# An encoder layer's step from recurrence to attention: one normalisation woven into the attention's maxima, with TensorE in program order from there

## The chip, the core and the metric

The kernel runs on one core of one Trainium2 chip. A core has TensorE (matrix products into PSUM; its weight loads are listed apart, as PEld), VectorE (DVE), ScalarE (ACT), GpSimd (POOL) and SyncE (SP), which issues most transfers. Each engine works off its own queue in order; semaphores join them. The metric is the device time of one execution in microseconds, lower is better.

## The reference

One layer of a hybrid encoder for 1024 prompt frames (positions 0 to 1023, no history) and 64 sample frames (with a recurrent state and 256 cached keys):

```python
proj = (rms_norm(x) * (1 + sc1) + sh1) @ w_in          # 1024 -> 3336 columns
r, k, v, decay, a, g = rwkv part of proj               # 8 heads x 64, token-shifted
y = rwkv_scan(...)                                     # delta rule, state 64 x 64 a head
mu, var = mean and variance of y over each head's 64 channels
y = (y - mu) * rsqrt(var + GN_EPS) * gn_g + gn_b
y_rwkv = (y + bonus) * g                               # g = sigmoid(dg) @ w_gate_up
q, kf, vf, logf = fox part of proj                     # 8 heads x 64
y_fox = softmax(q @ k.T / 8 + lc_q - lc_k, causal) @ v # lc: running sum of logf
x = x + gt1 * (concat(y_rwkv, y_fox) @ w_out)
x = x + gt2 * ((silu(h2 @ w_ffn_gate) * (h2 @ w_ffn_up)) @ w_ffn_down)
```

Everything is float32; most products are made of three products of a high and a low part.

## The kernel before, in words

Channels lie on the 128 partitions and frames along the free axis. Frames are worked in two halves (`halves`): the first has 512, the second 512 and the 64 samples. Eight heads are four pairs, `j` 0 to 3, two heads to a tile of 128 partitions.

`phase` makes the projections of a half and the recurrent part, in an order that a string (`ORDER`) writes out. `rwkv_b` (B) makes the recurrence: from one chunk of 64 frames to the next there is a chain of a matmul `pS` (L663) and two small evacuations of it, `sv` on VectorE (L666) and on ScalarE (L667); the outputs `pY` are copied into `y`, one head by ScalarE and one by VectorE (L672). `rwkv_n` (N, L677 on) normalises a pair: the mean by a matmul with `bmean` (`pbs`, L405), a subtraction on VectorE (L683), a square on ScalarE, the variance by another matmul, Ln and Exp on ScalarE, two operations of VectorE (L691, L692), the gate `g` by a matmul `plora` (L398), its product with `y` on VectorE (L693), and a DMA that GpSimd issues into the scratch `yscr` (L695). The pair 3 of the second half is the last; its normalisation stands behind the phase, as code of its own.

Attention follows. For each pair of heads of one half:

- `att_max` makes the approximate scores of each block of 128 queries against all keys that it may see (`pmx`, two halves of 512 keys at most, with a matmul of a mask `cmask` by the identity `identr` on the diagonal block) and takes their maxima on VectorE (L1022, `nmx` or `pc`). Its generator yields after each such piece.
- `att_rows` transposes the maxima (`pnm`, L1032) and writes them into rows of the query operand by two operations of VectorE, one a head (L1035), so that the scores come out with the maxima subtracted.
- `att_main` goes over the blocks of keys: the exact scores `pst` (two or three matmuls), Exp on ScalarE (L1064), sums over the blocks in `acc` (head 0 on VectorE, head 1 on GpSimd when `te.on` is set, L1077 to L1080), the products with the values `pav`, at the end the sum over keys `psm` and the division (L1147 to L1149). For samples there are the small `pss` and `pvs`.

`att_main` yields between its pieces, and the caller fills in pieces of other generators: the maxima of the next pair (`fill(mx, ...)`), the first half's attention (`low_steps`), the output projection `po`. `self.te` wraps TensorE: with `te.on` each matmul keeps the place that the code gives it; without, the scheduler may move it. In the profile its matmuls stand at L1906, its transposes at L1909. Before, `te.on` is set only in `att_second`, so the maxima and scores of pair 0 of the first half, and the maxima of pair 0 of the second half (both in `run`), are placed by the scheduler, between the recurrence's last steps and the last normalisation.

PSUM in this part has banks by tag: `mx` 2, `st` 3, `mm` 2, `pv` 1. For the first half's pairs 1 to 3 (`pair_bufs` with `big` false) the value products, the sums `psm` and the transposed maxima `pnm` share the two `mm` banks.

Operands of the first half's pairs lie in tiles that are free at that time: pair 1 in `mixfh`/`mixfl`, pair 2 in `mixrh`/`mixrl`, pair 3 in `mixr1`. GpSimd clears half of the rows of each (`aux_rows`, L890), then SyncE loads the rest (`pair_load`, L973). The rows of the second half's pair 1 are `kb1` and `q1`.

`att_consts` makes `identr`, two `cmask` and four `nmx` behind the phases: a cast on VectorE (L874), memsets and a select on GpSimd, two casts on VectorE (L883).

## Time and profile before

| | |
|---|---|
| runs, us | 1680.83, 1672.7, 1681.77 (median 1680.83) |
| the profiled execution: its own time, its span | 1676.35 us, 1674.7 us |
| mean granted clock of TensorE | 0.988 |
| TensorE busy | 1617.9 us, 97% of the span |
| VectorE, ScalarE, GpSimd busy | 63%, 39%, 12% |
| chain that ended last | TensorE 79%, VectorE 10%, ScalarE 5%, DMA 3% |

The recurrence's end, the last normalisation and pair 0 of the first half lie from about 660 to 700 us of the span, the second half's attention with the first half's pairs from 700 on, the output projection's filling from 786 on, and the rest of the layer behind 880. A table of windows gives for each stretch of the span the busy time of each engine, TensorE's granted clock (PEclk, 1 is full), the DMA engines' busy share and the rate. A table of waits gives who stood idle for whom: in total, how often, the longest. A timeline gives start, duration, engine, line, operation and, in brackets, the idle time ahead.

### The profile page before, as it was taken

The page shows a single profiled execution, that of the slowest core. Times are in us where ns is not written, and L with a number is a line of the kernel's source. Part 1 is how long each engine was busy: PE and PEld are TensorE (multiplying, and loading weights), DVE is VectorE, ACT ScalarE, POOL GpSimd, SP SyncE. Part 2 cuts the span into 40 slices and gives each one's busy share as a digit, 9 for nine tenths or more (in the row PEclk, how much of TensorE's full clock was granted, in tenths as well). Part 3 has the DMA queues.
Part 4 walks back from the last instruction along what each step waited for, and adds up shares of the span by engine and source line. Part 5 has one row for each costly group of instructions (what it writes and reads, how often), then busy time and mean ns, then how long its engine had stood idle before and what let it go on. Part 6 is the DMA issues. An engine that isn't in the chain of part 4 may idle for free.

```text
span 1674.7 us, 31845 instructions
## 1 busy us (share of the span) xinstructions
PE 1617.9 (97%) x12783; PEld 1397.8 (83%) x12783; DVE 1060.0 (63%) x2162; ACT 659.9 (39%) x1284; POOL 197.6 (12%) x336
## 2 busy tenths in 40 slices
PE   6999999999999999899999999999999999999999
PEld 3666777788888887555669899999999999999998
DVE  6576686757876653666668965555555556545545
ACT  4543565653545445234346632222333233211210
POOL 1101101030211013434441000000000000000000
PEclk9999999999999999899999999999999999999999
DMA  8535467531233244754434432222222226323313
GB/s 311 163 101 133 117 181 202 168 90 43 62 86 96 80 109 114 219 145 153 142 118 163 160 105 77 78 78 78 78 78 78 78 65 210 132 73 98 100 40 123
DMA packets 126738, 197.80 MB, mean 118 GB/s; under 512 B 60734, under 2 KB 67550, under 8 KB 126590
## 3 DMA queue, kind: packets, MB, share of 16 engines
q1 hardware_dynamic: 124862, 190.10, 37.3%
q0 software_dynamic: 1728, 5.67, 0.9%
q8 instruction: 100, 1.64, 0.4%
q14 instruction: 48, 0.39, 0.1%
HBM read 152.54 MB, written 43.19 MB: 117 GB/s over the span
## 4 chain that ended last, share of the span: by engine, by line
PE 79%; DVE 10%; ACT 5%; DMA 3%; issue 2%; SPq 1%; POOL 0%; DVEq 0%; ACTq 0%; POOLq 0%
PE pd L1548 16%; PE pfe L1433 8%; PE pfc L1433 8%; PE pfa L1433 8%; PE pmm L324 4%; PE pmm L326 4%; PE pfb L1433 4%; PE pmm L325 4%; PE po L1906 3%; PE pst L1906 2%; PE pbs L405 2%; PE pav L1906 2%; PE pmx L1906 2%; PE pS L663 1%; DVE wlo L246 1%
## 5 line engine op out<-in xcount | busy, mean ns | idle before, releaser
L324 PE MATMUL pmm<-hhi,whi 128*128 128x288 f32 (+1 forms) x624 | 218.7, 351 | 3.9 <-ACT pb L347 3.9
L325 PE MATMUL pmm<-hlo,whi 128*128 128x288 f32 (+1 forms) x624 | 216.6, 347 | 0.6 <-DVE hlo L302 0.6
L326 PE MATMUL pmm<-hhi,wlo 128*128 128x288 f32 (+1 forms) x624 | 213.5, 342 | 0.0
L242 ACT CAST whi<-wraw 128x1024 fp32r<-128x1024 f32 (+2 forms) x116 | 99.1, 855 | 222.3 <-PE pd L1548 165.0
L1548 PE MATMUL pd<-al,whi 128*128 128x512 f32 (+1 forms) x528 | 172.4, 327 | 0.0
L1548 PE MATMUL pd<-ah,wlo 128*128 128x512 f32 (+1 forms) x528 | 172.2, 326 | 0.0
L1548 PE MATMUL pd<-ah,whi 128*128 128x512 f32 (+1 forms) x528 | 172.2, 326 | 0.0
L1552 DVE SCALAR_TENSOR_TENSOR x1t<-pd,mod,x1t 128x512 f32<-128x512 f32 x192 | 91.4, 498 | 109.5 <-PE pd L1548 108.7
L324 PEld LDWEIGHTS pmm<-hhi,whi 128*128 128x128 f32 x624 | 119.1, 191 | 19.6 <-ACT pb L347 5.1
L325 PEld LDWEIGHTS pmm<-hlo,whi 128*128 128x128 f32 x624 | 119.1, 191 | 12.0 <-issue 1.7
L326 PEld LDWEIGHTS pmm<-hhi,wlo 128*128 128x128 f32 x624 | 118.6, 190 | 10.7 <-issue 1.7
L246 DVE TENSOR_TENSOR wlo<-wraw,whi 128x1024 fp32r<-128x1024 f32 (+2 forms) x108 | 104.8, 970 | 28.7 <-ACT whi L242 28.4
L1548 PEld LDWEIGHTS pd<-ah,whi 128*128 128x128 f32 x528 | 99.0, 188 | 7.1
L1548 PEld LDWEIGHTS pd<-ah,wlo 128*128 128x128 f32 x528 | 99.0, 188 | 7.1
L1548 PEld LDWEIGHTS pd<-al,whi 128*128 128x128 f32 x528 | 99.1, 188 | 7.0
L1433 PE MATMUL pfc<-hh,hS 128*128 128x256 f32 (+1 forms) x352 | 102.3, 291 | 1.2 <-ACT hh L1335 1.2
L1433 PE MATMUL pfc<-hh,lS 128*128 128x256 f32 (+1 forms) x352 | 102.3, 291 | 0.0
L1433 PE MATMUL pfa<-hh,whi 128*128 128x256 f32 (+1 forms) x352 | 101.8, 290 | 0.0
L1433 PE MATMUL pfa<-hl,whi 128*128 128x256 f32 (+1 forms) x352 | 101.8, 289 | 0.0
L1433 PE MATMUL pfa<-hh,wlo 128*128 128x256 f32 (+1 forms) x352 | 101.6, 289 | 0.0
L1433 PE MATMUL pfc<-hl,hS 128*128 128x256 f32 (+1 forms) x352 | 101.1, 287 | 0.0
L1380 ACT CAST hS<-wraw 128x512 fp32r<-128x512 f32 x88 | 53.6, 619 | 62.9 <-PE pfc L1433 62.0
(458 smaller groups left out, 4107.3 us busy)
## 6 DMA issues: line engine op xcount, KB each, us to landing
wraw<-in_w_in_dram SPq DMA_DIRECT2D x52, 512.0 KB
wada<-in_w_ada_dram SPq DMA_DIRECT2D x48, 512.0 KB
as<-actscr SPq DMA_DIRECT2D x22, 544.0 KB
wraw<-in_w_gate_dram SPq DMA_DIRECT2D x22, 512.0 KB
wraw<-in_w_up_dram SPq DMA_DIRECT2D x22, 512.0 KB
wraw<-in_w_down_dram SPq DMA_DIRECT2D x40, 256.0 KB
wraw<-in_w_out_dram SPq DMA_DIRECT2D x16, 512.0 KB
actscr<-sg SPq DMA_DIRECT2D x22, 288.0 KB
```

Of the source, the lines that this page charges most:

```text
L242: nc.scalar.copy(hi, src)
L246: eng.tensor_tensor(lo, src, hi.bitcast(F32), op=ALU.subtract)
L324: nc.tensor.matmul(ps[0:M, 0:n], whi[:, k, 0:M], xhi[:, k, off:off + n], start=(k == 0), stop=False)
L325: nc.tensor.matmul(ps[0:M, 0:n], whi[:, k, 0:M], xlo[:, k, off:off + n], start=False, stop=False)
L326: nc.tensor.matmul(ps[0:M, 0:n], wlo[:, k, 0:M], xhi[:, k, off:off + n], start=False, stop=(k == kt - 1))
L405: nc.tensor.matmul(ps[:, 0:n], w, x[:, off:off + n], start=True, stop=True)
L663: nc.tensor.matmul(ps, kb[:, c], sv[:, c], start=True, stop=True)
L1380: nc.scalar.copy(w[x][0], src)
L1433: nc.tensor.matmul(ps, l[:, k], r[:, s, k], start=(first and k == 0 and y == 0), stop=(k == 3 and y == 2), skip_group_check=True)
L1548: nc.tensor.matmul(ps[:, 0:n], w[:, i], x[:, t:t + n], start=(i == 0 and y == 0), stop=(i == len(fs) - 1 and y == 2))
L1552: nc.vector.scalar_tensor_tensor(dst, ps[:, so - off:so - off + l], self.mod[:, 40 + o, b:b + 1], dst, op0=ALU.mult, op1=ALU.add)
L1906: return self.pin(self.tc.nc.tensor.matmul(*a, **k))
```

## The change

The last normalisation becomes a generator, `rwkv_n_last`, whose three steps `run` takes at chosen places: the gate's product first (after the sixth piece of the first maxima), copied by ScalarE into a tile `glate`; then the mean and the square; then the variance and the rest. Its product with the gate goes from VectorE to GpSimd, and its matmuls go through `te`, in the `mm` banks. `te.on` is set at the end of the last phase, ahead of the first maxima. The maxima of the second half's pair 0 are filled in one a step (before: two after each whole block). In `rwkv_b` both heads of `y` of the last pair are copied by ScalarE. `att_consts` is called twice: inside the last phase for pair 0 of the first half, and behind the phases with three copies by ScalarE; its `nmx` are cleared by VectorE instead of GpSimd. For the first half's pairs the transposed maxima `pnm` take an `mx` bank instead of an `mm` one. In `low_steps` the next pair's maxima start one block sooner and come one a step, where they came two at a time. `mixfh` and `mixfl` are placed ahead of `mixrh` and `mixrl` in their pool.

```diff
@@ rwkv_b
-            for h, cp in enumerate((nc.scalar.copy, nc.vector.tensor_copy)):
+            for h, cp in enumerate((nc.scalar.copy, nc.scalar.copy if hf.smp and j == 3 else nc.vector.tensor_copy)):
...
+    def rwkv_n_last(self, hf, j, part, sgd):
...
+        def product(w, x):
+            for off, m in hf.chunks:
+                ps = self.ps([P, 512], tag="mm", name="pn3")
+                self.te.matmul(ps[:, 0:m], w, x[:, off:off + m], start=True, stop=True)
+                yield slice(off, off + m), ps[:, 0:m]
+        g = self.zpool.tile([P, 576], F32, tag="z", name="glate")
+        for c, ps in product(self.wg[:, j * P:(j + 1) * P], sgd):
+            nc.scalar.copy(g[:, c], ps)
+        yield
+        for c, ps in product(self.bmean, y):
+            nc.vector.tensor_tensor(y[:, c], y[:, c], ps, op=ALU.subtract)
+        rs = self.slot(name="gsq", tag="sb")
+        nc.scalar.activation(rs[:, 0:n], y[:, 0:n], AF.Square)
+        yield
+        for c, ps in product(self.bmean, rs):
+            nc.scalar.activation(rs[:, c], ps, AF.Ln, bias=self.eps_g)
+        nc.scalar.activation(rs[:, 0:n], rs[:, 0:n], AF.Exp, scale=-0.5)
+        nc.vector.scalar_tensor_tensor(y[:, 0:n], y[:, 0:n], col(V_GG), rs[:, 0:n], op0=ALU.mult, op1=ALU.mult)
+        nc.vector.scalar_tensor_tensor(y[:, 0:n], y[:, 0:n], col(V_GB), bon[:, 0:n], op0=ALU.add, op1=ALU.add)
+        nc.gpsimd.tensor_tensor(y[:, 0:n], y[:, 0:n], g[:, 0:n], op=ALU.mult)
+        self.late_q.dma_start(self.yscr[hf.i][:, j], y[:, 0:n])
+        yield
...
@@ att_consts
+        if src:
+            c["m"] = [ap.tile([P, 3 * P], F32R, name=f"cmask{x}") for x in range(2)]
+            for d, t in zip((c["id"], *c["m"]), (src["id"], *src["m"])):
+                nc.scalar.copy(d, t)
...
-            nc.gpsimd.memset(t, 0.0)
+            nc.vector.memset(t, 0.0)
...
@@ pair_bufs
-                                                {"pv": "mm", "sm": "mm", "dn": "mm"})
+                                                {"pv": "mm", "sm": "mx", "dn": "mm"})
...
@@ low_steps
-                    fill(mx, 2 * (last > 1))
+                    fill(mx, last > 0)
...
                 else:
+                    fill(mx, last > 0)
                     last = b + 1
...
@@ run
-            for b, f in late.values():
-                f(b())
...
-            for _ in self.att_max(0, halves[0], self.g0):
-                pass
+            self.te.on = True
+            (n3,) = late.values()
+            mx, fill = self.att_max(0, halves[1], g), lambda n: [next(mx, None) for _ in range(n)]
+            for i, _ in enumerate(self.att_max(0, halves[0], self.g0)):
+                if i == 5:
+                    next(n3)
             self.att_rows(0, halves[0], self.g0)
-            mx, fill = self.att_max(0, halves[1], g), lambda n: [next(mx, None) for _ in range(n)]
             for b in self.att_main(0, halves[0], self.g0):
-                fill(2 if isinstance(b, int) else 1 if b != "v" else 99)
+                if b in (0, 1, 2):
+                    next(n3, None)
+                fill(1 if b != "v" else 5)
+            fill(99)
...
-            mine = {x: rows4(p, halves[0], x) for x in ("mixrh", "mixrl", "mixfh", "mixfl")}
+            mine = {x: rows4(p, halves[0], x) for x in ("mixfh", "mixfl", "mixrh", "mixrl")}
```

The order of the instructions moves at three places of which the prediction speaks. (The lines' numbers differ between the two programs: L1948 and L1951 after are L1906 and L1909 before, both inside the `te` wrapper.) The first is TensorE at the end of pair 0's first maxima; `kbf`, `qf`, `kaf`, `qaf` are the first half's operands, `kb` and `q` the second half's, `z` and `wg` make the gate. Before:

```order
L1906 MATMUL pmx<-kbf,qf 128x512
L405 MATMUL pbs<-gsq,bmean 128x288
L1906 MATMUL pmx<-cmask_8106,identr 128x256
L405 MATMUL pbs<-gsq,bmean 128x288
L1909 MATMUL pnm<-ident,nmx_8117 64x128
L398 MATMUL plora<-z,wg 128x288
L1906 MATMUL pst<-qf,kbf 128x512
L1906 MATMUL pst<-cmask_8114,identr 128x256
```

After, from the same `pnm` on:

```order
L1951 MATMUL pnm<-ident,nmx_7563 64x128
L1948 MATMUL pst<-qaf,kaf 128x512
L1948 MATMUL pst<-qf,kbf 128x512
L1948 MATMUL pst<-cmask_7560,identr 128x256
L1948 MATMUL pmx<-kb_8112,q_8113 128x512
L1948 MATMUL pst<-qaf,kaf 128x512
L1948 MATMUL pst<-qf,kbf 128x512
L1948 MATMUL pst<-cmask_7560,identr 128x256
L1948 MATMUL pmx<-kb_8112,q_8113 128x256
L1948 MATMUL pmx<-cmask_8096,identr 128x256
L1948 MATMUL pn_8213<-y,bmean 128x288
L1948 MATMUL pn_8216<-y,bmean 128x288
```

The normalisation's products (`pbs` before, `pn` after) no longer stand between the first maxima; they come behind the first scores, with the second half's maxima between them.

The second place is TensorE in the first half's pair 2, where the maxima of pair 3 (`pmx` from `mixr`) are filled in between its scores (`pst` from `mixrl` and `mixrh`). Before, behind the scores of blocks 0 and 1:

```order
L1906 MATMUL pmx<-mixr_8365 128x256
L1906 MATMUL pmx<-cmask_8106,identr 128x256
L1906 MATMUL pmx<-mixr_8365 128x256
L1906 MATMUL pmx<-cmask_8106,identr 128x256
L1906 MATMUL pst<-mixrl_8382 128x256
L1906 MATMUL pst<-mixrh_8381 128x256
L1906 MATMUL pst<-cmask_8114,identr 128x256
L1906 MATMUL pmx<-mixr_8365 128x384
L1906 MATMUL pmx<-cmask_8106,identr 128x256
L1906 MATMUL pmx<-mixr_8365 128x512
L1906 MATMUL pmx<-cmask_8106,identr 128x256
L1909 MATMUL pnm<-ident,nmx_8120 64x128
```

After, from the scores of block 1 (384 wide) on:

```order
L1948 MATMUL pst<-mixrl_8394 128x384
L1948 MATMUL pst<-mixrh_8393 128x384
L1948 MATMUL pst<-cmask_8097,identr 128x256
L1948 MATMUL pmx<-mixr_8375 128x256
L1948 MATMUL pmx<-cmask_8096,identr 128x256
L1948 MATMUL pst<-mixrl_8394 128x384
L1948 MATMUL pst<-mixrh_8393 128x384
L1948 MATMUL pst<-cmask_8097,identr 128x256
L1948 MATMUL pmx<-mixr_8375 128x256
L1948 MATMUL pmx<-cmask_8096,identr 128x256
L1948 MATMUL pmx<-mixr_8375 128x384
L1948 MATMUL pmx<-cmask_8096,identr 128x256
```

The maxima begin at block 1 instead of block 2, mostly one at a time.

The third place is GpSimd between the clearing of pair 3's rows (`mixr`) and that of the second half's pair 1 (`kb`). Before:

```order
L890 MEMSET mixr_8365 64x1024 x2
L1077 COPY acc<-pt 128x128 x2
L695 DMA yscr_72<-y 128x576
L890 MEMSET mixfh_8383 64x1024 x2
L890 MEMSET mixrh_8381 64x1024 x2
L890 MEMSET kb_8407 64x2688
```

After:

```order
L924 MEMSET mixr_8375 64x1024 x2
L1113 COPY acc<-pt 128x128 x2
L1114 TENSOR_TENSOR acc<-pt 128x384
L1116 TENSOR_TENSOR acc<-acc,pt 128x256
L723 TENSOR_TENSOR y<-y,glate 128x576
L724 DMA yscr_72<-y 128x576
L1116 TENSOR_TENSOR acc<-acc,pt 128x128
L924 MEMSET mixfh_8391 64x1024 x2
L924 MEMSET mixrh_8393 64x1024 x2
L924 MEMSET kb_8417 64x2688
```

Three additions of head 1 (`te.on` now holds for them) and the product with the gate stand ahead of the clearing that the loads of pair 1 and of `kb1` wait for.

On VectorE the cast of `identr` (L874), which stood between the fourth and fifth `sv` of the last recurrence, goes to pair 2's recurrence some 60 us earlier; in its place stand four memsets of 128x64. On ScalarE three copies (128x128 and twice 128x384) and one copy of `y` come in at the same point.

More of the change, by code (lines that the diff above doesn't have):

```diff
@@ L695, in rwkv_n @@
         self.late_q.dma_start(self.yscr[hf.i][:, j], y[:, 0:n])
+    def rwkv_n_last(self, hf, j, part, sgd):
+        nc, vc, n = self.nc, self.vc, hf.n
+        col = lambda base: vc[:, base + j:base + j + 1]
+        y, bon = part
+        def product(w, x):
[20 more added lines that the diff above has]
+        yield
     def ones_rows(self):
@@ L869, in cache_kv, with att_consts @@
         self.put_split(kf, j, SP + SS, PAST, 1)
-    def att_consts(self, ap):
+    def att_consts(self, ap, n, src=None):
         nc = self.nc
-        self.identr = ap.tile([P, P], F32R, name="identr")
-        nc.vector.tensor_copy(self.identr, self.ident)
-        self.cmask = []
-        for x in range(2):
+        c = {"id": ap.tile([P, P], F32R, name="identr"), "m": []}
+        if src:
+            c["m"] = [ap.tile([P, 3 * P], F32R, name=f"cmask{x}") for x in range(2)]
+            for d, t in zip((c["id"], *c["m"]), (src["id"], *src["m"])):
+                nc.scalar.copy(d, t)
+        else:
+            nc.vector.tensor_copy(c["id"], self.ident)
+        for x in range(0 if src else 2):
             cm = self.slot([P, P], name="cm")
@@ L880, in att_consts @@
                                     pattern=[[2 * x - 1, P]], channel_multiplier=1 - 2 * x)
-            self.cmask.append(ap.tile([P, 3 * P], F32R, name=f"cmask{x}"))
-            nc.gpsimd.memset(self.cmask[x].bitcast(F32), 0.0)
-            nc.vector.tensor_copy(self.cmask[x][:, P:2 * P], cm)
-        self.nmx = [ap.tile([P, 64], F32, name=f"nmx{x}") for x in range(4)]
-        for t in self.nmx:
-            nc.gpsimd.memset(t, 0.0)
+            c["m"].append(ap.tile([P, 3 * P], F32R, name=f"cmask{x}"))
+            nc.gpsimd.memset(c["m"][x].bitcast(F32), 0.0)
+            nc.vector.tensor_copy(c["m"][x][:, P:2 * P], cm)
+        c["nmx"] = [ap.tile([P, 64], F32, name=f"nmx{x}") for x in range(n)]
+        for t in c["nmx"]:
+            nc.vector.memset(t, 0.0)
+        return c
     def aux_rows(self, kb, *rest):
@@ L921, in pair_bufs @@
     def pair_bufs(self, g, big):
+        g["c"] = self.ac
         for n, m in (("pt", 512), ("acc", 512), ("r", 512), ("fy", 576)):
@@ L1001, in att_max @@
         nc, te = self.nc, self.te
-        nmx = self.nmx[2 * hf.i + j % 2]
+        c_ = g["c"]
+        nmx = c_["nmx"][(2 * hf.i + j % 2) % len(c_["nmx"])]
         kb, qc = g["kb"], g["q"]
@@ L1017, in att_max @@
                         e, m2 = (0, SS) if smp else (max(0, d - P), 256)
-                        te.matmul(ps[0:qn, e:e + m2], self.identr[0:qn, 0:qn],
-                                  self.cmask[0][0:qn, P - d + e:P - d + e + m2], start=False, stop=True,
+                        te.matmul(ps[0:qn, e:e + m2], c_["id"][0:qn, 0:qn],
+                                  c_["m"][0][0:qn, P - d + e:P - d + e + m2], start=False, stop=True,
                                   skip_group_check=True)
@@ L1031, in att_rows @@
         pt = self.ps([64, P], tag=g["tags"]["sm"], name="pnm")
-        te.transpose(pt, self.nmx[2 * hf.i + j % 2], self.ident)
+        te.transpose(pt, g["c"]["nmx"][(2 * hf.i + j % 2) % len(g["c"]["nmx"])], self.ident)
         for h in range(2):
@@ L1060, in scores @@
                 if diag:
-                    te.matmul(ps[:, w:w + 256], self.identr, self.cmask[1][:, P - c0 + w:P - c0 + w + 256], start=False,
+                    te.matmul(ps[:, w:w + 256], g["c"]["id"], g["c"]["m"][1][:, P - c0 + w:P - c0 + w + 256], start=False,
                               stop=True, skip_group_check=True)
@@ L1111, in att_main @@
                     te.matmul(ps[:, h, x], kb[h][:, kc], qb[h][:, 512:576], start=False, stop=x < 2, skip_group_check=True)
-                te.matmul(ps[:, h, 2], self.identr, self.cmask[1][:, P:P + SS], start=False, stop=True,
+                te.matmul(ps[:, h, 2], g["c"]["id"], g["c"]["m"][1][:, P:P + SS], start=False, stop=True,
                           skip_group_check=True)
@@ L1614, in phase @@
             r[j] = (lambda p=p: p, lambda p, j=j: self.rwkv_n(hf, j, p, zg))
-        return r
+        return {j: self.rwkv_n_last(hf, j, p, zg) for j, p in y.items()} if hf.smp else r
     def run(self):
@@ L1706, in early @@
                 rws.close()
-                self.g0 = self.pair_first(E(at0, "att0"))
+                p = E(at0, "att0")
+                self.ac = self.att_consts(p, 1)
+                self.g0 = self.pair_first(p)
                 for x in range(2):
@@ L1737, in run @@
             with tc.high_priority():
-                self.att_consts(R(att, "attc", 1))
+                self.ac = self.att_consts(R(att, "attc", 1), 4, self.ac)
             self.pkeys = {}
```

3 lines of the change are left out of this document (1 added, 2 removed).

## The prediction

> **What bounds the kernel now.** I read the page first.
>
> ```profile
> span 1674.7 us, 31845 instructions
> PE 1617.9 (97%) x12783; PEld 1397.8 (83%) x12783; DVE 1060.0 (63%) x2162; ACT 659.9 (39%) x1284; POOL 197.6 (12%) x336
> ```
>
> TensorE is busy 97% of the span, so the change, which adds no product and takes none away, can only win idle time of TensorE or time at a lower clock. Where those lie, a table of windows around the change tells (time, then busy time of TensorE, its weight loads, VectorE, ScalarE, GpSimd; granted clock; DMA share; GB/s).
>
> ```profile
> 600.00:665.90 65.90, 65.31 (x641) 56.17 (x641) 25.03 (x49) 35.51 (x83) 10.31 (x12) 1.00 0.42 111
> 665.90:700.10 34.20, 26.80 (x125) 16.60 (x123) 25.59 (x55) 10.65 (x25) 21.30 (x31) 0.97 0.71 193
> 700.10:711.20 11.10, 10.01 (x38) 8.28 (x39) 5.59 (x12) 2.88 (x5) 0.96 (x1) 0.64 1.04 277
> 711.20:734.20 23.00, 22.60 (x121) 15.30 (x122) 17.94 (x34) 8.35 (x17) 8.76 (x10) 1.00 0.42 130
> 734.20:766.00 31.80, 25.46 (x134) 14.41 (x133) 16.95 (x33) 12.53 (x27) 7.94 (x10) 0.89 0.52 154
> 766.00:880.00 114.00, 112.66 (x593) 78.26 (x593) 71.26 (x93) 45.76 (x88) 52.76 (x44) 1.00 0.43 141
> ```
>
> Ahead of 665.9 and behind 766 TensorE is full (65.31 of 65.90; 112.66 of 114.00). Between them it idles 34.20 - 26.80 = 7.4 us in the second row and 31.80 - 25.46 = 6.3 us in the fifth, and the clock falls in the second, third and fifth. What is won there passes on to the end, because the work behind is TensorE's own. Next the waits of TensorE, from 665 to 712 and then from 712 to 768 (total, times, longest), the small ones left out:
>
> ```profile
> PE pS L663 <- ACT sv L667: 2.5, 2, 2.2
> PE pmx L1906 <- DVE pc L1022: 1.5, 4, 0.7
> PE pss L1906 <- DVE q L1035: 0.8, 1, 0.8
> PE pnm L1909 <- DVE nmx L1025: 0.7, 1, 0.7
> ```
>
> ```profile
> PE pmx L1906 <- DVE nmx L1022: 2.2, 5, 0.7
> PE psm L1906 <- DVE mixr L1035: 1.6, 1, 1.6
> PE psm L1906 <- DVE mixrh L1035: 1.0, 1, 1.0
> PE pnm L1909 <- DVE nmx L1022: 0.8, 1, 0.8
> PE pss L1906 <- DVE nmx L1022: 0.8, 1, 0.8
> ```
>
> It is VectorE that ends nearly every one: its maxima and the rows made of them. Last, the windows in which the clock was at half:
>
> ```profile
> 697.90:708.10 10.20, 8.70 (x32) 7.44 (x33) 4.95 (x12) 1.68 (x3) 0.00 (x0) 0.50 1.04 245
> 749.10:752.50 3.40, 3.40 (x10) 0.98 (x10) 1.64 (x2) 0.00 (x0) 0.00 (x0) 0.50 0.41 89
> 759.30:762.70 3.40, 3.40 (x13) 2.25 (x14) 0.58 (x2) 1.82 (x4) 1.04 (x1) 0.50 0.79 236
> ```
>
> Each follows a run of waits. At half clock half of the busy time is lost: 4.35, 1.7 and 1.7 us.
>
> **Part by part.** *The masks.* The rows: VectorE's casts, GpSimd's memset, TensorE's `pS` behind them.
>
> ```profile
> 665.46 2.25 DVE L874 CAST identr<-ident 128x128 fp32r<-128x128 f32 x1
> 671.53 0.21 DVE L883 CAST cmask<-cm 128x128 fp32r<-128x128 f32 x1
> 665.29 2.33 POOL L890 MEMSET kb<- 64x2688 f32 x1 [11.87 <-PE pmm L326]
> 668.41 0.49 PE L663 MATMUL pS<-sv,kr 128*128 128x128 f32 x2 [2.24 <-ACT sv L667]
> 728.29 0.49 ACT L1064 ACTIVATE pt<-pst 128x384 f32<-128x384 f32 x1 [4.72 <-PE pst L1906]
> 728.88 0.28 ACT L1064 ACTIVATE x<-pst 128x128 f32<-128x128 f32 x1
> ```
>
> Two casts of one shape took 2.25 and 0.21 us; the long one began during GpSimd's memset and ended 0.09 us behind it (667.71 against 667.62), and the recurrence stood 2.24 us for it. The cast goes. ScalarE takes three copies in its place, by its nearest rows 0.28 + 2 x 0.49 = 1.26 us, ahead of the next `sv`, so I keep 1.0 us of 2.24. Bounds: 2.2 if ScalarE's gaps hide the copies; 1.0 us lost if the four new memsets of VectorE stand behind GpSimd's as the cast did. I take **-1.0**. The earlier masks, 60 us ahead, lie beside TensorE's projections (first row above) and cost nothing; uncovered, they would be one GpSimd memset, about 1 us. The Trainium skill (SBUF — State Buffer, Who interferes with whom) says that casts and copies of VectorE in two-port modes, and its operations with two SBUF inputs against GpSimd's reads, wait for GpSimd's whole instruction, while a VectorE memset does not on trn2; the cast agrees, no row here shows the memset. By it the memsets are free and the term stays.
>
> *First maxima, normalisation, second maxima.* Of the 7.4 us idle 2.5 were the recurrence; 4.9 are left. The normalisation's steps now lie between scores and maxima, so neither VectorE nor TensorE meets them in the chain; VectorE also loses two copies of `y`, the product with the gate and head 1's additions. The two `psm`, which stood apart, become neighbours:
>
> ```profile
> 688.87 1.07 PE L1906 MATMUL psm<-acc,ones 128*64 128x512 f32 x2
> 735.47 1.08 PE L1906 MATMUL psm<-x,ones 128*64 128x512 f32 x4 [0.99 <-DVE mixrh L1035]
> 693.55 0.68 DVE L1149 TENSOR_TENSOR fy<-pav,r 128x512 f32<-128x512 f32 x1
> ```
>
> One head alone took 1.07, both together 1.08, so 1.0 us of TensorE goes. The tail stays: the last maximum to `pnm` 0.7, to the rows 0.8, and `fy` (0.68) now comes between the two rows; with 0.6 that I leave for small waits for VectorE, 2.8 stay. So 4.9 + 1.0 - 2.8 = **-3.1**; bounds 0 (the pinned queue meets as many waits as it had) and -5.2.
>
> *The first half-clock stretch.* 4.35 us; with fewer waits ahead of it I let one third of its length come back: **-2.9**, bounds 0 and -4.35.
>
> *GpSimd and the loads.* Three additions and the gate's product come ahead of the clearing of `mixfh`, `mixrh` and `kb1`, and SyncE's queue stands behind that.
>
> ```profile
> 758.95 1.40 POOL L246 TENSOR_TENSOR mixfl<-fy,mixfh 128x576 fp32r<-128x576 f32 x1 [2.30 <-ACT mixfh L242]
> 687.37 1.84 POOL L890 MEMSET mixfh<- 64x1024 f32 x2
> 694.73 1.12 SPq L973 DMA_DIRECT2D kb<-kx  x2
> 711.23 0.47 PE L1906 MATMUL pmx<-kb,q 128*128 128x512 f32 x1
> mixfl<-qx SPq DMA_DIRECT2D x1, 512.0 KB
> v<-vtok SPq DMA_DIRECT2D x2, 512.0 KB
> q<-qx SPq DMA_DIRECT2D x3, 288.0 KB
> kb<-kx SPq DMA_DIRECT2D x3, 672.0 KB
> ```
>
> The clearing follows `y`'s last product, before and after. That product takes 1.40 us on GpSimd by its nearest row, and its steps, behind two scores now, come some 1.6 us later: together 3, so the clearing starts near 690.4 instead of 687.37 and `kb1` is issued near 698 instead of 694.73. How long a load then takes is in no row; the transfers were saturated (1.04) at 277 GB/s, and from `mixfl` (two of 512 KB) over `v` and `q1` to `kb1` 2.5 MB are issued, some 9 us, so I estimate that `kb1` landed near 700 and will land near 703.5. TensorE needs it at 711.23 now, without a wait, and 7 to 8.5 us sooner then (the terms above): 703 to 704. A wait of **+1.0**, bounds 0 and 4. The other order of the tiles in their pool has its price in the same term.
>
> *One block sooner, and the `mx` bank.* 6.3 us idle in the fifth row: 2.2 + 0.8 + 0.8 for maxima that came two at a time with two banks, 1.6 and 1.0 for `psm`, which stood until VectorE had read `pnm` out of the other `mm` bank. Spread singly, most of the first go; in an `mx` bank `pnm` holds up nobody that comes within 1.4 us. 0.7 stays, and 1.0 comes new in pair 1, where VectorE is busy 17.94 of 23.00 us and gets more maxima: **-4.6**, bounds -2 and -6.
>
> *The other two half-clock stretches.* They follow these waits: 3.4 us, of which I take **-2.6**, bounds 0 and -3.4.
>
> Sum: -1.0 - 3.1 - 2.9 + 1.0 - 4.6 - 2.6 = -13.2 us. The profiled execution took 1676.35 us, 1.65 above its span; that gives 1663.1. It lies 4.5 below the median of the three runs and inside them (1672.7 to 1681.77); the mean of the four is 1677.9, and from that I forecast **1665**.
>
> **Rivals.** *The clock does not follow.* The stretches began at 697.9, 749.1 and 759.3: 51.2 and 10.2 us apart, 15 and 3 times 3.4, and they last 10.2, 3.4 and 3.4. So the gate looks at fixed pieces of 3.4 us, and ahead of the first the waits were small, at most 1.5 us (the first table's four of `pmx`). If such small waits suffice, those that I leave do too: no clock term, -13.2 + 5.5 = -7.7, and without the load's wait -8.7: 1669. The Trainium skill (TensorE: Matmul & The Clock Gate, What's actually happening) gives the same window, 3413 ns, free-running, but throttles after an idle window; none of these was idle, so the trace agrees with the length and not with the condition. By its rule idle gaps this short would decide nothing, and the time would be the same 1669. Chance 0.22.
>
> *The loads become the bound: slower.* GpSimd's additions and VectorE's two-input operations stand for each other:
>
> ```profile
> 723.24 1.45 DVE L1080 TENSOR_TENSOR x<-x 128x256 f32<-128x256 f32 x1
> 733.45 0.42 DVE L1080 TENSOR_TENSOR acc<-acc,pt 128x256 f32<-128x256 f32 x1
> 720.61 0.29 PE L1906 MATMUL pmx<-mixrh 128*128 128x256 f32 x1
> ```
>
> The same addition took 1.45 beside GpSimd's and 0.42 alone. Four such meetings ahead of the clearing put it past 694, `kb1` to 709 and `mixrh` behind it to 716, while TensorE, pinned, wants them at 703 and 711: it stands 6 and 5 us with everything queued behind, and the clock falls again as often as now, with one piece more (1.7). -1.0 - 3.1 + 11 - 4.6 + 1.7 = +4: 1682. It decides if the first clearing of `mixfh` begins later than 694. For it: the saturated queue; against: no wait on a load now, with 11 us to spare at `kb1`. Chance 0.10.
>
> *The gains are given back.* The pinned order meets a wait of VectorE at nearly each maximum (bounds 0 and -2 of the two idle terms), clocks half won: -1 - 2 + 1 = -2: 1676. Chance 0.10.
>
> **How the numbers follow.** The forecast keeps 0.58, with 1656 to 1671 of its own: its best bounds (-2.2 - 5.2 - 4.35 - 6 - 3.4 = -21) give 1657 from the mean, its worst reach the rivals. The range 1656 to 1676 adds the clock's rival and half of the last. A measurement can tell about 0.5%, 8.4 us: faster means below 1669.5. The forecast lies there but for 0.04, and of the clock's rival 0.13 of its 0.22: 0.67 faster. Slower than 1686.3 is the far side of the loads' rival, with 0.05. The rest, 0.28, is the same.
>
> **What would show it.** Right: `pS` with no wait over 1.3 us; the first `pss` from `q` and `kb` near 696; half-clock time under 8 us in place of 17; no wait of `psm` for L1035; TensorE busy over 95% from 734 on. Wrong: a wait of `pmx` for a load of `kb1` or `mixrh` over 4 us; the clearing of `mixfh` behind 694; idle time from 665 to 766 still over 10 us.

## The result and the profile after

The changed kernel takes 1667.38 us (median of 15 executions), the kernel before 1677.53 (15 executions): a ratio of 0.994, interval 0.9928 to 0.9952, 10.2 us less. Two of the fifteen executions of the changed kernel took 3879 us, at a granted clock of 1.00 in their records; no profile of them is kept, so their cause is open, and the ratio and its interval leave them out. 1665 was forecast, 1656 to 1676 as the range. The profiled execution of the changed kernel is one of 1667.38 us. Its page begins:

```profile
span 1665.7 us, 31855 instructions
PE 1610.5 (97%) x12783; PEld 1396.0 (84%) x12783; DVE 1056.6 (63%) x2159; ACT 662.4 (40%) x1292; POOL 202.5 (12%) x336
```

TensorE makes the same 12783 products and is busy 7.4 us less, in a span that is 9.0 us shorter: most of the gain is not idle time, but products that ran faster or stood closer. The table of windows of the changed kernel, with edges at the same products as the six rows of the prediction (columns as there):

```profile
600.00:667.76 67.76, 66.87 (x656) 57.54 (x657) 26.33 (x58) 35.57 (x85) 11.75 (x15) 1.00 0.45 117
667.76:697.99 30.23, 23.29 (x125) 15.86 (x125) 21.44 (x44) 13.04 (x31) 22.44 (x25) 1.00 0.69 186
697.99:710.90 12.91, 10.58 (x41) 8.23 (x42) 7.72 (x16) 3.44 (x6) 2.40 (x4) 0.74 1.04 285
710.90:732.42 21.52, 20.49 (x109) 14.00 (x111) 15.47 (x31) 8.32 (x18) 8.10 (x9) 1.00 0.47 181
732.42:758.35 25.93, 23.94 (x146) 14.22 (x141) 17.11 (x32) 10.80 (x24) 7.98 (x10) 0.93 0.59 166
758.35:873.45 115.10, 112.92 (x594) 78.20 (x593) 72.93 (x95) 46.82 (x90) 53.08 (x44) 1.00 0.44 140
```

The second row lost 4 us and the fifth 5.9; the third, at half clock for half of its length (0.74), became longer (12.91 for 11.10), and still has 2.3 us of idle time. Idle time in rows two to five is 6.94 + 2.33 + 1.03 + 1.99 = 12.3 us, where it was 7.4 + 1.1 + 0.4 + 6.3 = 15.2. TensorE's waits from 660 to 712, and then from 705 to 768 (total, times, longest):

```profile
PE pnm L1951 <- DVE nmx L1058: 2.9, 3, 1.3
PE pS L663 <- ACT sv L667: 1.8, 2, 0.9
PE pss L1948 <- DVE q L1071: 1.5, 2, 0.9
PE pmx L1948 <- DVE pc L1058: 1.0, 2, 0.7
PE pmx L1948 <- DVE mixfh L1071: 0.7, 1, 0.7
```

```profile
PE pmx L1948 <- DVE nmx L1058: 1.5, 4, 0.7
PE pnm L1951 <- DVE nmx L1058: 1.4, 2, 1.1
PE pss L1948 <- DVE nmx L1058: 0.8, 1, 0.8
```

The 2.2 us wait of `pS` and both of `psm` are gone; `pnm` and `pss` wait longer than before. Last the clock: two stretches at half are left of three, each with the piece of 3.41 us ahead of it:

```profile
696.29:699.70 3.41, 1.47 (x11) 1.25 (x11) 2.70 (x4) 0.64 (x2) 2.78 (x4) 1.00 1.04 410
699.70:706.53 6.83, 6.82 (x24) 5.73 (x25) 2.68 (x7) 1.69 (x3) 0.05 (x1) 0.50 1.05 259
750.90:754.32 3.42, 2.64 (x20) 2.23 (x19) 2.10 (x4) 2.77 (x8) 0.56 (x2) 1.00 0.32 79
754.32:757.73 3.41, 3.41 (x14) 1.29 (x14) 2.19 (x3) 1.29 (x3) 1.31 (x1) 0.50 0.90 299
```

The stretch near 700 is 6.8 us (10.2 before), all of it busy; those at 749 and 759 became one of 3.4.

For all kernels below I measure one stretch between two products that every one of them makes: from the recurrence's 130th `pgT` (655.04 us of the span before, 656.90 after) to the second product of `po` (786.69 and 780.13). It took 131.65 us before and 123.23 after: 8.4 us less. The time outside it changes from run to run by the clock: ahead of that `pgT` the fourteen profiles of this study have between 10.2 and 30.7 us at half clock (20.5 before, 23.9 after), and it comes between 651.1 and 659.0 us. A difference of 2 or 3 us between two total times says little here; the stretch says more. But each kernel has one profile, and one half-clock piece more or less (1.7 us) can come by chance in the stretch too: the changed kernel and the first two runs below have the same products up to the second half's `pnm`, the same idle time there (6.1 us), and took 39.8, 41.4 and 41.4 us to it, because in the last two a piece of 3.41 us at half clock fell into it.

| kernel | median us (executions) | ratio to before, interval | stretch, us | idle in it | half clock in it |
|---|---|---|---|---|---|
| before | 1677.53 (15) | | 131.65 | 15.4 | 17.1 |
| changed | 1667.38 (15) | 0.994, 0.9928 to 0.9952 | 123.23 | 13.3 | 10.2 |
| wide products in the waits | 1663.35 (6) | 0.9915, 0.9887 to 0.9943 | 122.52 | 11.9 | 6.8 |
| narrow products in the waits | 1666.20 (10) | 0.9936, 0.9916 to 0.9957 | 123.27 | 11.3 | 10.2 |
| sooner maxima and bank alone | 1672.79 (12) | 0.9979, 0.9956 to 1.0002 | 126.97 | 13.2 | 13.6 |
| without these two | 1674.93 (12) | 0.9983, 0.9963 to 1.0002 | 126.90 | 15.4 | 13.6 |
| maxima two at a time, later | 1671.16 (1) | | 127.17 | 14.7 | 13.6 |
| `pnm` in an `mm` bank | 1663.72 (1) | | 125.30 | 15.2 | 10.2 |
| normalisation first | 1676.80 (1) | | 134.51 | 17.4 | 23.9 |
| masks late | 1669.15 (1) | | 124.09 | 13.6 | 10.2 |
| own tile for the last state | 1663.09 (5) | 0.9917, 0.9901 to 0.9932 | 122.51 | 12.6 | 10.2 |
| woven further | 1661.06 (6) | 0.992, 0.9893 to 0.9946 | 117.26 | 8.9 | 6.8 |
| the same, wide products | 1659.93 (6) | 0.9904, 0.988 to 0.9928 | 121.46 | 12.1 | 6.8 |
| the same, loads sooner | 1657.65 (6) | 0.9884, 0.986 to 0.9907 | 118.11 | 9.5 | 3.4 |

### The profile page after: what moved, and what is told of

The parts are those of the page before. It is cut to its first block, busy times and chain, and to the rows that moved or that the text cites. A ratio compares the mean times of both kernels' runs of the same rounds, so it can differ in the third digit from the quotient of the medians.

```text
span 1665.7 us, 31855 instructions
## 1 busy us (share of the span) xinstructions
PE 1610.5 (97%) x12783; PEld 1396.0 (84%) x12783; DVE 1056.6 (63%) x2159; ACT 662.4 (40%) x1292; POOL 202.5 (12%) x336
## 4 chain that ended last, share of the span: by engine, by line
PE 80%; DVE 9%; ACT 4%; DMA 3%; issue 2%; SPq 1%; POOL 0%; DVEq 0%; ACTq 0%
PE pd L1584 16%; PE pfe L1469 8%; PE pfc L1469 8%; PE pfa L1469 8%; PE pmm L326 4%; PE pmm L324 4%; PE pmm L325 4%; PE pfb L1469 4%; PE po L1948 3%; PE pst L1948 2%; PE pbs L405 2%; PE pav L1948 2%; PE pmx L1948 2%; PE pS L663 1%; DVE wlo L246 1%
```

## The experiments

**What the clock follows.** Products that nothing reads were put into the waits around the samples' small scores, once with 512 columns and once with 64. Theory A, columns; theory B, idle time; theory C, neither.

```diff
             ps = self.ps([P, 2, 3, SS], tag=tags["sm"], name="pss")
+            more = self.ps([P, 512], tag="mm", name="pmore") if j < 2 else None
             for h in two:
+                for _ in range(((4, 2), (3, 0))[j][h] if j < 2 else 0):
+                    te.matmul(more[:, 0:512], ka[0][:, 0:P], qa[0][:, 0:512], start=True, stop=True)
```

(With narrow products: 7, 5 and 6 of them, and 64 for 512.)

> The changed kernel, with products of 512 columns that nothing reads put into TensorE's waits around the samples' small scores: four behind pnm and two between the heads for the second half's pair 0, three for its pair 1. Theory A (the clock follows the columns that TensorE streams in a piece of 3.4 us; in the traces of before and after nearly every piece under about 2,700 columns was followed by one at half clock, those above were not): the piece of the first pss has 669 columns now and gets some 3,700, the one of pair 1 has 2,610 and gets 4,100; the half-clock stretches near 700 (6.8 us) and 754 (3.4 us) go. The products cost nothing in the first wait (0.85 us in 0.91), at most 0.4 us in all, so 4.6 - 0.4 = 4 us less than the changed kernel: 1663. Theory B (the idle waits of a piece decide): the same stretches go, since the waits are filled. Theory C (the clock follows neither here): both stretches stay and the time is that of the changed kernel or 0.4 more, 1667 to 1668.

> As the run with wide products, but with products of 64 columns, as many as fill the same time: seven and five for pair 0, six for pair 1. TensorE is as busy as with the wide ones, and streams few columns. Theory A: the piece of the first pss gets 12 x 64 columns, some 1,440 in all, still far under 2,700: half clock near 700 stays at 6.8 us; pair 1's gets 2,610 + 384 = 2,990 and is in doubt; time 1667 to 1668, at best 1666. Theory B: the idle time of these pieces is gone, both stretches go, 1663. Theory C: 1667 to 1668 with both stretches.

Measured: 1663.35 and 1666.20. First the wide products, windows of 3.41 us from 692.77 on and, after "...", those from 703.01 on:

```profile
692.77:696.18 3.41, 2.83 (x15) 1.60 (x12) 2.25 (x5) 1.23 (x2) 3.41 (x3) 1.00 0.95 308
696.18:699.59 3.41, 3.26 (x22) 2.78 (x22) 1.88 (x6) 1.09 (x2) 0.79 (x3) 1.00 1.08 320
...
703.01:706.42 3.41, 1.09 (x5) 0.75 (x5) 2.64 (x5) 0.42 (x1) 1.26 (x1) 1.00 1.05 208
706.42:709.83 3.41, 3.41 (x12) 2.72 (x11) 1.75 (x4) 1.79 (x3) 0.29 (x1) 0.50 1.05 331
```

The pieces of the first `pss` stream 4,203 and 4,502 columns (the columns of the products' outputs, summed over the timeline, a product over an edge shared by time) and nothing at half clock follows. A new half-clock piece stands behind the one at 703.01, with 1,397: in it TensorE, sooner here, waits 1.04 us for maxima and then 1.28 us for the load of `kb1`. Then the narrow ones:

```profile
693.60:697.01 3.41, 2.71 (x20) 1.93 (x17) 2.25 (x5) 1.23 (x2) 3.22 (x2) 1.00 0.96 328
697.01:700.43 3.42, 3.42 (x17) 3.32 (x17) 0.92 (x2) 0.41 (x1) 0.75 (x2) 0.50 1.08 309
700.43:703.84 3.41, 3.41 (x12) 2.64 (x10) 1.70 (x5) 1.27 (x3) 0.00 (x0) 0.50 1.00 267
```

The middle piece has no idle time at all, 3.42 of 3.42 us busy, and the clock stays at half behind it. What ran in it, TensorE's timeline:

```profile
697.23 1.25 PE L1951 MATMUL pmore<-opr,opr 128*128 128x64 f32 x5
698.30 0.40 PE L1951 MATMUL pss<-opr 128*128 128x64 f32 x1
698.51 0.40 PE L1951 MATMUL pss<-q,kb 128*128 128x64 f32 x1
```

Products of 64 columns, 1,357 columns in all. (Busy is what the profile counts as busy; the products lie one behind the other without a gap.) The pieces ahead, the first row of each fence, idle nearly the same, 0.58 and 0.70 us, but stream 4,203 and 2,156 columns, and only the second is followed by half clock. The grid of the pieces lies alike against the second half's `pnm` in both runs, within 0.3 us, so its place does not explain the difference. B falls by these pieces, C by the other run; A stands. From the second half's `pnm` to pair 1's it took 12.28 us in the changed kernel, 12.19 with narrow products and 9.59 with wide ones: 2.7 us from the clock and the filled waits, of which pair 1's part gives back 1.9 by the load and the half clock behind it.

In pair 1 the narrow run's half-clock piece went too. Its piece there streamed 3,649 columns, where the changed kernel's had 2,610: 384 more are the six products, the rest comes from where the grid fell, so it is not shown that the six did it. I then summed the columns of every 3.41 us piece between 675 and 790 us in all fourteen profiles (471 pieces): all 36 under 2,650 were followed by half clock, 5 of the 9 between 2,650 and 3,000, none of the 426 above. Idle time does not sort them: of 93 pieces at full clock that idled 0.7 us or more, 26 were followed by half clock. The limit of 2,650 is read off these profiles themselves. From 660 to 675, in the recurrence, the rule is weaker: five pieces with 1,668 to 1,920 columns passed at full clock, one with 1,614 did not. Its products have plain float32 operands, the attention's are fp32r; whether that counts was not tried.

**The halves of the change apart.** The two edits in `low_steps` and `pair_bufs`, alone on the kernel before, and the changed kernel without them:

```diff
-                    fill(mx, 2 * (last > 1))
+                    fill(mx, last > 0)
...
                 else:
+                    fill(mx, last > 0)
                     last = b + 1
...
-                                                {"pv": "mm", "sm": "mm", "dn": "mm"})
+                                                {"pv": "mm", "sm": "mx", "dn": "mm"})
```

> The kernel before with two edits alone: the first half's next maxima one block sooner and one a step, and pnm in an mx bank. The prediction gave them 4.6 us of waits and 2.6 us of half clock: 7.2 us less than before, 1670; the stretches at 749 and 759 go. By the trace of the changed kernel the stretch from the first half's pair 2 to the end of pair 3 gained 4.8 us (of these 1.7 half clock): 1673. Rival: these edits won only because the ones ahead had moved the start: nothing, 1677.

> The changed kernel without the sooner maxima and without the mx bank for pnm: masks, normalisation, pinned first maxima alone. The prediction gave these 1.0 + 3.1 + 2.9 - 1.0 = 6.0 us: 1671.5. By the trace of the changed kernel the part up to the second half's first scores gained 4.0 us and the first half-clock stretch nothing: 1673. If the two halves of the change add up, its gain and that of the run with the two edits alone sum to 10.1 us.

Measured: 1672.79 and 1674.93, both with intervals that reach 1.0002. In the stretch each half is worth 4.7 us (131.65 to 126.97 and to 126.90), together 9.4, where the whole change has 8.4: they nearly add up. In the total times they do not (3.1 and 0.9 us under the 1675.86 of before on that chip, 4.0 where 10.1 was the sum to expect); the profiles of these two have 27.3 and 30.7 us at half clock ahead of the stretch. It is not the profiled execution alone: over its twelve the second has a median granted clock of 0.986, before 0.988 over 27 and the changed kernel 0.989. Taking from each execution the share of its span that the clock lost (an estimate from these figures, the clock known to 0.001, 1.7 us), the two lie 1.6 and 3.5 us under before. Why the second loses more to the clock outside the stretch is open.

**The two edits of the lower half.** One undone at a time in the changed kernel (the fences above, read backwards: the first two for the maxima, the last for the bank).

> The changed kernel with the first half's next maxima two at a time and one block later, as before; pnm keeps the mx bank. Theory: the waits of pmx (2.2), pnm (0.8) and pss (0.8) in the first half's pair 2 come back in part: from the first psm of pair 1 to that of pair 2 the trace took 23.2 us, 29.5 before; 25 to 26 here, with one half-clock piece more in or behind it. Rival (the bank did it): 23.2 to 24.

> The changed kernel with pnm of the first half's pairs back in an mm bank; the maxima stay sooner and one a step. Theory: the two waits of psm (1.0 and 1.6 us) behind the rows come back, and the wait of 0.68 us of pmx for the rows of pair 1, new with the mx bank, goes: 2 us more from pair 1's pnm to the second output product, 71.1 us in the changed kernel, 73 here. Rival (with the maxima sooner, pnm is over before psm comes): no psm wait, and 0.7 us less than the changed kernel.

Measured: from `psm` to `psm` 27.9 us without the sooner maxima (23.2 in the changed kernel), more than the 25 to 26 expected, since it has 6.8 us at half clock there; so the maxima are worth 3.9 us of the stretch (by one profile of each kernel). With `pnm` in an `mm` bank the part from pair 1's `pnm` on took 73.24 us (71.15), as expected. TensorE's waits of that run:

```profile
PE psm L1948 <- DVE mixr L1071: 1.6, 1, 1.6
PE pmx L1948 <- DVE nmx L1058: 1.5, 4, 0.7
PE psm L1948 <- DVE mixrh L1071: 1.0, 1, 1.0
```

Both waits of `psm` are back to the tenth. The bank's price stands in the changed kernel, in pair 1, a row that this run lacks:

```profile
710.93 0.36 PE L1948 MATMUL pmx<-kb,q 128*128 128x256 f32 x1 [0.68 <-DVE mixfh L1071]
```

The maximum waits for the `mx` bank until VectorE has read `pnm` out of it. The run's one time, 1663.72, is below the changed kernel's although its stretch is 2.1 us longer: it has only 10.2 us at half clock ahead of it.

**The normalisation and the masks.**

```diff
             (n3,) = late.values()
+            for _ in n3:
+                pass
```

> The changed kernel with the three steps of the last normalisation taken one after the other ahead of the first maxima, instead of woven into the scores. Theory (the prediction's): weaving hides the steps' chain of VectorE and ScalarE; in a row, TensorE stands for the subtraction (0.94), the square (0.69) and their starts, some 2 us, and the first maxima come later. From the recurrence's product at 656.9 to the pnm of the second half's pair 0 it took 39.8 us; 42 to 43 here, without any change behind that. Rival: the scheduler's place of the steps was no cost, since VectorE's maxima end the same wait: 39.8 again.

From the `pgT` to the second half's `pnm` it took 51.6 us (39.8 in the changed kernel), not the 42 to 43 expected. The waits of the normalisation's products up to there (others left out at "..."):

```profile
PE pn L1950 <- ACT glate L711: 2.3, 1, 2.3
...
PE pn L1950 <- ACT gsq L716: 1.3, 1, 1.3
...
PE pY L670 <- ACT y L672: 0.8, 1, 0.8
PE pn L1950 <- ACT y L672: 0.5, 1, 0.5
```

The chain stands bare: idle time 4.5 us above the changed kernel's, and 13.7 us at half clock came with it where there were none. I had counted 2 to 3 us of waits and nothing for the clock.

```diff
-                self.ac = self.att_consts(p, 1)
+                self.ac = None
...
-                self.ac = self.att_consts(R(att, "attc", 1), 4, self.ac)
+                self.ac = self.g0["c"] = self.att_consts(R(att, "attc", 1), 4)
...
-            nc.vector.memset(t, 0.0)
+            nc.gpsimd.memset(t, 0.0)
...
-            for h, cp in enumerate((nc.scalar.copy, nc.scalar.copy if hf.smp and j == 3 else nc.vector.tensor_copy)):
+            for h, cp in enumerate((nc.scalar.copy, nc.vector.tensor_copy)):
```

> The changed kernel with the masks made once, behind the phases, as before (cast by VectorE, clearing by GpSimd), and with VectorE's copies of the last pair's y. Theory: the wait of 2.24 us of the recurrence for the cast that stands for GpSimd's memset comes back and the one of 0.89 us for ScalarE's three copies goes: from the recurrence's product to the pnm of the first half 21.5 us in the changed kernel, 22.5 to 23 here. Rival: the cast meets no memset of GpSimd at its new time, and the recurrence has no wait at all: 20.6.

Measured: 22.7 us to the first `pnm` (21.5), as expected. VectorE's cast, GpSimd's memset and the recurrence, each from its engine's timeline:

```profile
666.00 2.25 DVE L908 CAST identr<-ident 128x128 fp32r<-128x128 f32 x1
665.83 2.33 POOL L924 MEMSET kb<- 64x2688 f32 x1 [11.87 <-PE pmm L326]
668.96 0.49 PE L663 MATMUL pS<-sv,kr 128*128 128x128 f32 x2 [2.23 <-ACT sv L667]
```

The same cast met the same memset and took the same 2.25 us. Early masks, with `y`'s copy on ScalarE, are worth 1.3 us.

**A wait that the change brought.** VectorE and GpSimd of the changed kernel; the same of the kernel before:

```profile
676.97 0.28 DVE L666 TENSOR_SCALAR state<-pS,pc 64x64 f32<-64x64 f32 x1 [1.08 <-DMA out_state_p_dram<-state]
673.99 0.54 POOL L658 DMA_DIRECT2D out_state_p_dram<-state  x1 [0.35 <-ACT state L667]
```

```profile
675.26 0.27 DVE L666 TENSOR_SCALAR state<-pS,pc 64x64 f32<-64x64 f32 x1
672.57 0.72 POOL L658 DMA_DIRECT2D out_state_p_dram<-state  x1
```

The last state of the samples is written over the prompt's, whose transfer GpSimd issues. The recurrence itself lies 1.86 us later in the changed kernel's span, so the times have to be counted from its `pgT`. So counted the transfer is not issued later, as I held when I wrote the expectation below, but sooner: 17.09 us behind it, for 17.53. It lands at 19.97, for 19.42, since it takes 2.88 us and not 1.89; three other transfers are issued just ahead of it now, but that they slow it is not shown. And VectorE comes to the write at 18.99 now; before it came at 20.22, with the transfer over. So VectorE stands 1.08 us, with two maxima queued behind, and TensorE's `pnm` stands 1.3 us for those.

```diff
                     put_state(8, st)
+                    S1 = self.rpool.tile([P, 64], F32, tag="st1", name="state_e")
...
-                s0, s1 = (S[hsl[0]], S[hsl[1]]) if last else (sv[hsl[0], c + 1, 0], sv[hsl[1], c + 1, 1])
+                So = S1 if c == 8 else S
+                s0, s1 = (So[hsl[0]], So[hsl[1]]) if last else (sv[hsl[0], c + 1, 0], sv[hsl[1], c + 1, 1])
...
-            self.late_q.dma_start(O["state_s"][j], S)
+            self.late_q.dma_start(O["state_s"][j], S1)
```

> The changed kernel with a tile of its own for the samples' last state, so that VectorE need not wait for the transfer of the prompt's state out of the same tile. In the changed kernel this wait (1.08 us at 676.97, not there before, because GpSimd issues the transfer at 673.99 instead of 672.57) stands ahead of the last two maxima, and pnm waits 1.32 us. Theory: the wait goes, pnm waits 0.3 to 0.6 us, TensorE gains 0.8 to 1.0 us up to that pnm (21.5 us from the recurrence's product, 20.5 here), and the half clock that followed this piece in some runs does not; time 1665 to 1666.5 where the changed kernel has 1667.4. Rival: the reductions were bound by the two mx banks anyway, and nothing is gained.

VectorE's wait is gone, `pnm` waits 0.9 (0.3 to 0.6 expected; that the gate's products ahead of the last maxima keep it so is argued). TensorE's idle time up to it fell from 3.8 to 3.0 us. The part up to it took 22.2 us, of which 3.4 at half clock, where none was expected; without that loss of 1.7 it is the 20.5 expected. The time, 1663.09, is lower than the stretch explains (0.7 us); in the profile the rest lies ahead of it, with 13.7 us at half clock for 23.9.

**A version that beats both.** Besides the own tile, all tried together only: the gate's products behind the last maximum, the copies of the masks without priority, pair 1's `pnm` in an `mm` bank, and the first scores begun ahead of the small ones (`begin` makes a score's first product, which `scores` then skips).

```diff
-                if i == 5:
+                if i == 7:
                     next(n3)
...
-            with tc.high_priority():
-                self.ac = self.att_consts(R(att, "attc", 1), 4, self.ac)
+            self.ac = self.att_consts(R(att, "attc", 1), 4, self.ac)
...
+            gs[1]["tags"]["sm"] = "mm"
...
+            for h in two:
+                begin(0, 0, h)
             ps = self.ps([P, 2, 3, SS], tag=tags["sm"], name="pss")
             for h in two:
+                if h:
+                    begin(1, 0, 0)
```

> The changed kernel with five edits: the samples' last state has its own tile; the gate's products come behind the last of the first maxima instead of ahead of it; the copies of the masks are not ahead of the recurrence by priority; pnm of pair 1 of the first half takes an mm bank (free then), the others an mx bank; and in the second half the first products of the first scores (512 columns each) are begun ahead of and between the samples' small scores. No work is added. Expected against the changed kernel: wait of the first pnm 1.3 to 0.3 (-1.0), wait of pmx for the rows of pair 1 (-0.7), waits of pss 1.5 to 0.9 and 0.8 to 0.4 (-1.0), half clock behind the first pss (some 2,200 columns instead of 669, under the 2,700 of theory A, so in doubt) 0 to -3: 2.7 to 5.7 less, 1662 to 1664.7. Rival: the products that fill the waits push the maxima behind them later, and nothing is won: 1667.

> As the run before, and products of 512 columns that nothing reads: two ahead of each head's small scores in pair 0 and one in pair 1. Theory A: the piece of the first pss streams over 3,700 columns, the half clock behind it goes for sure; four products of 0.21 us lie in what is left of the waits (0.9): 1661 to 1662, up to 3 less than the run before where that one kept the half clock, else the same. Theory C: 0.2 to 0.6 more than the run before.

Measured: 1661.06 and 1659.93. The first shortens the stretch by 6.0 us, somewhat over the 2.7 to 5.7 expected; its 6.8 us of half clock near 691 stay, behind 2,525 columns. In the second they go (4,181 to 5,116 columns in the pieces of the small scores), and TensorE, sooner by that, meets a wait of its own kind, so that its stretch is 4.2 us longer than the first's. TensorE's and SyncE's timelines:

```profile
705.86 0.77 PE L1966 MATMUL pmx<-kb,q 128*128 128x512 f32 x1 [4.11 <-DMA kb<-kx]
694.49 1.11 SPq L1010 DMA_DIRECT2D kb<-kx  x2
```

The load of `kb1`, issued at 694.49, landed at 705.9, taking the end of the wait for the landing: 11.4 us later. 6.8 us of half clock followed. The woven kernel without the wide products waits 0.22 us at that place. Counted from `pgT` TensorE comes there 1.8 us later in it, and its load, issued at the same point (39.85 us behind `pgT`, 39.63 here), takes 9.05 us; why it takes 2.3 longer here is open. So the load goes ahead of `v`:

```diff
             self.pair_ops(attp, self.high)
+            self.aux_rows(self.mixhi[0].a[:, 0:2], self.mixhi[0].a[:, 2:4])
...
             for x in (1, 2):
                 self.pair_load(0, h1, g, x)
                 self.pair_load(1, h0, gs[1], x)
+                if x == 1:
+                    self.pair_load(1, h1, self.pair_get(1), 0)
             self.att_rows(0, h1, g)
-            self.pair_load(1, h1, self.pair_get(1), 0)
```

(`pairs_low` no longer clears `mixrh`.)

> The woven kernel with the wide products, and the second half's pair 1 fetched sooner: its loads q and kb go ahead of the values' load v (some 700 KB), and GpSimd clears its rows ahead of the last of mixrh. In the woven kernel with the wide products pmx of that pair waited 4.1 us for this load, issued at 694.5 and landed at 705.9, while the transfers were saturated (277 to 284 GB/s), and 6.8 us at half clock followed. Theory (the load's rival of the prediction, now in force): kb lands 2.5 to 4 us sooner, the wait falls under 1.5 us, the half clock behind it to 3.4 us or none: 3 to 6 less in the stretch from the pnm of pair 1 to that of pair 2 (29.3 us there, 23 to 26 here), time 1654 to 1657 against 1659.9. Rival: the values then come too late for the second half's products with them, or the bandwidth only moves the wait to mixfl or v: 28 to 30 in that stretch, 1659 to 1661.

```profile
702.31 0.77 PE L1969 MATMUL pmx<-kb,q 128*128 128x512 f32 x1 [1.63 <-DMA kb<-kx]
692.48 1.12 SPq L1011 DMA_DIRECT2D kb<-kx  x2
```

Its wait is 1.63 us, a little over the 1.5 expected, the part from `pnm` to `pnm` 26.0 us for 29.3, just inside the 23 to 26 expected; the time is 1657.65, ratio 0.9884 (0.986 to 0.9907), below the changed kernel's interval. It is not shown to beat the woven kernel: their intervals overlap (0.9893 to 0.9946 there), and by the stretch the woven one, which makes no product that nothing reads, is 0.9 us shorter (117.26 for 118.11).

## Why the prediction was right, and where not

The time came out 2.4 us above the forecast, by the way of the forecast: waits for VectorE and part of the clock. That it came so near is in part luck: of the 13.2 us forecast, all of them in the stretch, 8.4 came, and the other 1.8 of the 10.2 us lie outside it, where nothing was forecast. By its own steps, in the stretch (8.4 us for 13.2):

- *The masks*, -1.0: measured -1.3 by the run with late masks. The recurrence waits 0.89 us behind ScalarE's three copies, as bounded, and 0.90 more behind a cast of `wraw` on ScalarE, which I had not seen. The Trainium skill (SBUF — State Buffer, Who interferes with whom) lets a VectorE memset on trn2 run beside GpSimd; no row of before could show it. The rows of VectorE and GpSimd of the changed kernel agree: the four take 0.11 us each, and the last two begin after GpSimd's memset of 2.33 us:

```profile
667.03 0.33 DVE L919 MEMSET nmx<- 128x64 f32 x4 [0.52 <-PE pmm L325]
667.15 2.33 POOL L924 MEMSET kb<- 64x2688 f32 x1 [11.87 <-PE pmm L326]
```

- *Masks, first maxima and normalisation*, -4.1 together: the parts up to the second half's `pnm` went from 23.78 + 19.98 to 21.47 + 18.35 us, -3.9. Right in sum; inside it, the transfer that VectorE waits for (1.08) was a step that I had not followed to its landing.
- *The first half-clock stretch*, -2.9, and *the loads*, +1.0: the part from `pnm` to `pnm` went from 12.07 to 12.28 us, +0.2 instead of -1.9. This is the step that failed. I held that fewer waits ahead of the stretch let a third of it come back. The piece of 3.41 us ahead of it streamed 669 columns, since the small scores and the waits around them fill it, and no removal of waits ahead of that changes it. One piece of three went, 0.9 us by busy time (4.35 lost before, 3.4 now), and `pss` waits 0.61 us for head 1's row behind `fy`, which the prediction had put into its tail and not onto `pss`. The load cost nothing: TensorE wanted `kb1` at 709.31 and not at 703, counted from `pgT` 3.8 us sooner than before and not 7 to 8.5. It was issued at 698.72, as forecast (698):

```profile
709.31 0.47 PE L1948 MATMUL pmx<-kb,q 128*128 128x512 f32 x1
698.72 1.11 SPq L1008 DMA_DIRECT2D kb<-kx  x2
```

- *One block sooner and the bank*, -4.6, and *the other half-clock stretches*, -2.6: pair 1's part is +0.1, the part behind it 51.2 to 46.5 us, together -4.7 instead of -7.2. `psm` lost its 2.6 us of waits as forecast, and 0.68 came new in pair 1 for the 1.0 forecast. The other waits are the second term that was mis-sized: of 4.0 us of idle time behind pair 1, for `pmx`, `pnm` and `pss`, 0.7 were to stay and 3.0 stay; and of 3.4 us of clock loss 1.7 went.
- Of the 8.4 us, 2.1 are idle time, 2.7 half clock by busy time, 1.0 the paired `psm`; the last 2.6 are shorter busy time of the other products, which I did not follow one by one.

*The rivals.* That the clock does not follow was half true, and for another reason than small waits. The Trainium skill (TensorE: Matmul & The Clock Gate, What's actually happening) has the gate follow how busy TensorE has lately been and throttle behind an idle window; the fully busy piece at 697.01 of the narrow run, with the clock at half behind it, speaks against busy time, as the profile counts it, as the measure. The loads' rival did not come, and its point of decision was wrong: the clearing of `mixfh` began at 691.4, before its 694, but how soon TensorE wants `kb1` and how long the load takes count as well. With the clearing 4.7 us sooner still (686.7) the woven kernel with the wide products waited 4.1 us. The gains given back: no.

*The marks.* Right: `pS` waits 0.9 at most, `psm` waits for no row, the first `pss` with `kb` comes 4.0 us sooner behind the recurrence's product (41.1 for 45.1; at 698.0 of the span, not near 696), no load is waited for. Wrong: half clock 10.2 us, not under 8; TensorE busy 92% from 732 to 758, not 95; idle time of 12.3 us still over 10, which the prediction had named as a sign against it.

## What to carry to other kernels

Look at TensorE in pieces of the clock's grid and count columns, not idle time: a group of small products beside a wait costs a half-clock piece (up to 1.7 us here, 3.4 where the next is narrow too), and wide products between them keep it away. Here products that nothing reads did so; those that are due anyway, begun sooner in the woven kernel, brought 2,525 columns and were not enough. When a step moves to another engine or time, follow that engine's queue to the end, its transfers included: a write that VectorE reached 1.2 us sooner met a transfer that landed 0.55 us later, and cost VectorE 1.08 us and TensorE 0.8 us of idle time. Count times from a product that both kernels make, not from the start of the span. Where the clock makes the total time vary by several us, compare a stretch between two products that both kernels make, and keep in mind that a half-clock piece can come or stay away in it by where the grid falls; a load with time to spare in one kernel is the bound of the next.

## What the runs showed that I had not expected

- The clock's threshold in the attention part: 36 of 36 pieces under 2,650 columns in 3.41 us were followed by half clock, none of 426 above 3,000, whatever their idle time; a completely busy one with 1,357, itself at half clock, was.
- The half clock ahead of the changed part varies between 10.2 and 30.7 us a run in the profiles, which is up to 10 us of time; the 27 executions of before beside the first runs lie 13.7 us apart (1672.39 to 1686.13), so it can be most of that spread, not all.
- A load of 672 KB landed 11.4 us after its issue with 249 GB/s moving in that time, where I had estimated 5 to 6 from the bytes queued ahead.
